# A list scheduler writes the order of all engines up to LayerNorm 1, and part of the second modulation is summed beside the FFN's first blocks

## The chip, the cores and the metric

The kernel runs on one core of a Trainium2 chip. Its time is the device time of one execution in microseconds, the median over runs. The engines of the core are named as in the profile: PE (TensorE, matrix products and transposes, with PEld for its weight loads), DVE (VectorE), ACT (ScalarE), POOL (GpSimd) and SP (SyncE, which issues all DMA transfers here). Each engine takes its instructions in the order in which the program lists them for it, and waits at an instruction whose inputs are not there.

## The reference

One layer of a diffusion transformer, in float32, for 256 latent tokens and 256 context tokens of width 2048. A conditioning vector gives six modulation vectors of width 2048 each (`w_ada` is 2048 x 12288, 100 MB). With one layer, the context only gives keys and values.

```python
sh1, sc1, g1, sh2, sc2, g2 = ada_mods(c, w_ada[layer], b_ada[layer])
csh1, csc1, ... = ada_mods(c_ctx[None, :], w_ada[layer], b_ada[layer])
qa, ka, va, qb, kb, vb = mixer_qkv(modulate(x, sh1, sc1), w_in[layer], ..., rope)
...
heads = concatenate([window_sink_attention(qa, ka, va, kac, vac, sink_logit[layer]),
                     global_attention(qb, kb, vb, kbc, vbc)], axis=-1)
x = layer_norm(DN_ALPHA * x + g1 * (heads @ w_out[layer]), ln1_g[layer], ln1_b[layer])
x = layer_norm(DN_ALPHA * x + g2 * swiglu(modulate(x, sh2, sc2), w_gate[layer], w_up[layer],
                                         w_down[layer]), ln2_g[layer], ln2_b[layer])
```

There are 16 query heads of 128 (8 windowed with a sink, 8 global with normalised queries and keys), 4 key/value heads, and an FFN of width 5632.

## The kernel before

**Products.** Every large product is made of three float32r matmuls (`mm3`, lines 130 to 133): a number is split into a rounded part `hi` and a rest `lo`, and hi x hi, hi x lo and lo x hi are summed. Weights come as raw float32 tiles of [128, 4 x 512] (1 MB) by SP; ACT rounds them (`hi`, line 121), DVE subtracts (`lo`, line 122), each 1024 columns at a time. A raw tile sits in one of six buffers up to LayerNorm 1 (four of `wraw`, two of `araw`), four afterwards. Inputs are split in the same way: `uh`/`ul` (modulated input), `oTh`/`oTl` (attention output), `u2h`/`u2l` (FFN input), `hTh`/`hTl` (FFN hidden).

**Modulation.** Modulation vectors are w_ada^T silu(c) in two ways. On PE, `ada_steps` multiplies raw float32 tiles by the conditioning columns into a bank `adaps` (line 230; a float32 matmul is two records in the trace), ACT copies it, and a tiny product with `sel` (line 253, the column step) turns rows into per-partition columns. On DVE, `ada_vector_steps` multiplies and adds raw tiles into an accumulator (line 204), 512 or 1024 columns at a time, and PE sums the partitions with a product with `ones` (line 268 for the gate g1 or g2, line 602 for columns).

**Stages.** (1) The input's 16 k-chunks of 128 are taken in groups of 1, 1, 2, 4 and 8 (`GROUPS`). `prep(g)` loads both halves of w_ada for the group, makes shift and scale, transposes x and ctx (line 351), modulates (line 355), and splits; `in_steps(g)` multiplies with w_in in six blocks of 512 columns and adds to q, k and v. `merge` interleaves the steps of group g with `prep(g+1)` evenly. Groups 0 and 1 load w_in as two tiles of 1536 columns each. (2) Keys, queries, and `attend_steps` for four head groups, merged with the rest of w_in, with the gate g1's DVE sums, and with `out_block`s, the products with w_out. (3) The second modulation feeds the FFN's input. It comes in four pieces of 512: m0 on DVE beside the last output blocks, m1 (shift and scale) on PE beside and after them (`first_modulation`), m2 and m3 on DVE beside the FFN's first blocks. (4) LayerNorm 1, then `z_part` transposes and modulates two k-chunks at a time. The FFN's gate and up blocks f = 0 to 5 are first done for k-chunks 0 to 7 only (`first_half`, 24 steps of 24 matmuls; the sums are put aside in `spill`) while m2 and m3 are summed; then they are finished, then f = 6 to 10. (5) The down projection, LayerNorm 2.

**What sets the order.** Lists are merged in Python, and from there the tile framework's own scheduler orders each engine's instructions, SP's included. Only two places are `manual_schedule` regions, where an engine takes the order of the code: ACT and DVE at the very start, and DVE, ACT and PE from the last output block to the FFN's first step.

## Time and profile before

| what | value |
|---|---|
| median of 3 runs | 1188.52 us (1187.82 to 1192.65) |
| profiled execution, its own time | 1189.62 us |
| its span, first to last instruction | 1187.8 us |
| granted PE clock, mean | 0.992 |
| read from HBM over the span | 289.91 MB |

The trace has several views. The table of stages gives each engine's busy time in a stretch of the span, with the number of instructions, the granted PE clock (1.00 is full), the mean busy share of the 16 DMA engines, and GB/s. The chain of waits goes back from the last instruction to what released it, piece by piece. The timeline has one row for each instruction or run of like ones: start, length, engine, line, operation, out<-in, count, and in brackets the idle time before it and what ended it. SPq rows are DMA issues. Matmul records are as long as a matmul's whole passage through the array, so two of them overlap; what one costs is the distance between starts.

### The profile page before, as it was taken

To read this page: it belongs to the slowest core of one execution; us is meant where nothing else is said; L and a number is where in the kernel's file an instruction comes from. 1 tells how busy PE (TensorE), PEld (TensorE's weight loads), DVE (VectorE), ACT (ScalarE), POOL (GpSimd) and SP (SyncE) were. 2 spreads that over 40 slices of the span, in tenths; PEclk is the share of its full clock that TensorE was granted. 3 is DMA by queue.
4 is the path that set the end of the run, shared out by engine and by line. 5 is a ranking of instruction groups with operands and counts; after the bars stand their busy time and mean duration, and the time that the engine had idled before them with its cause. 6 is when DMAs were issued, how large, how long until landed. Compare 5 with 4: busy or idle time off the path is not lost.

```text
span 1187.8 us, 14248 instructions
## 1 busy us (share of the span) xinstructions
PE 1158.3 (98%) x5527; PEld 916.4 (77%) x5527; DVE 800.4 (67%) x1026; ACT 530.3 (45%) x762; POOL 21.1 (2%) x43
## 2 busy tenths in 40 slices
PE   8999899999999999999999999999999999999995
PEld 7666578867777768888888888888888888888884
DVE  3763289998867888775776564544545778676556
ACT  2443142668675245445544444444444434343340
POOL 1100000000000010100000000000000000000000
PEclk9999999999999999999999999999999999999997
DMA  9999878853565969998675555565565888877541
GB/s 300 375 390 375 333 272 311 297 203 108 171 214 205 309 231 348 335 314 291 212 230 177 182 196 190 180 205 183 180 208 184 313 317 318 288 256 253 200 139 71
DMA packets 150137, 292.93 MB, mean 247 GB/s; under 512 B 5515, under 2 KB 20267, under 8 KB 147765
## 3 DMA queue, kind: packets, MB, share of 16 engines
q1 hardware_dynamic: 150070, 292.03, 70.8%
q8 instruction: 43, 0.70, 0.2%
q14 instruction: 24, 0.20, 0.0%
HBM read 289.91 MB, written 2.10 MB: 246 GB/s over the span
## 4 chain that ended last, share of the span: by engine, by line
PE 92%; DVE 3%; DMA 2%; ACT 1%; SPq 1%; issue 0%; DVEq 0%; ACTq 0%
PE acc L132 27%; PE acc L133 27%; PE acc L131 27%; PE adaps L230 3%; PE wk L537 2%; DMA raw<-in_w_ada_dram 2%; PE wk L525 1%; DVE lo L122 1%; PE wk L820 1%; PE wk L131 1%; PE wk L133 1%; PE wk L132 1%; PE wk L268 1%; SPq L101 1%; DVE xt L927 0%; PE wk L602 0%
## 5 line engine op out<-in xcount | busy, mean ns | idle before, releaser
L122 DVE TENSOR_TENSOR lo<-raw,hi 128x1024 fp32r<-128x1024 f32 x344 | 415.9, 1217 | 252.1 <-ACT hi L121 247.8
L121 ACT CAST hi<-raw 128x1024 fp32r<-128x1024 f32 x344 | 358.0, 1048 | 470.5 <-PE acc L133 406.2
L131 PE MATMUL acc<-hi,u2h 128*128 128x512 f32 x704 | 275.9, 392 | 0.8 <-ACT u2h L782 0.7
L133 PE MATMUL acc<-hi,u2l 128*128 128x512 f32 x704 | 274.9, 391 | 1.3 <-DVE u2l L783 1.3
L132 PE MATMUL acc<-lo,u2h 128*128 128x512 f32 x704 | 274.7, 390 | 0.0
L133 PEld LDWEIGHTS acc<-hi,u2l 128*128 128x128 f32 x704 | 132.6, 188 | 29.3 <-DVE u2l L783 1.7
L131 PEld LDWEIGHTS acc<-hi,u2h 128*128 128x128 f32 x704 | 132.6, 188 | 28.2 <-ACT u2h L782 1.2
L132 PEld LDWEIGHTS acc<-lo,u2h 128*128 128x128 f32 x704 | 132.6, 188 | 27.0
L131 PE MATMUL acc<-hi,hTh 128*128 128x512 f32 x344 | 135.5, 394 | 0.0
L133 PE MATMUL acc<-hi,hTl 128*128 128x512 f32 x344 | 134.1, 390 | 0.0
L132 PE MATMUL acc<-lo,hTh 128*128 128x512 f32 x344 | 134.0, 390 | 0.0
L204 DVE SCALAR_TENSOR_TENSOR adav<-raw,cs,adav 128x512 f32<-128x512 f32 (+1 forms) x112 | 109.5, 977 | 13.1 <-DMA raw<-in_w_ada_dram 11.5
L132 PE MATMUL acc<-lo,uh 128*128 128x512 f32 x256 | 102.0, 399 | 2.4 <-DVE lo L122 2.4
L131 PE MATMUL acc<-hi,uh 128*128 128x512 f32 x256 | 99.5, 405 | 2.8 <-ACT hi L121 2.8
L133 PE MATMUL acc<-hi,ul 128*128 128x512 f32 x256 | 101.4, 396 | 0.0
L132 PEld LDWEIGHTS acc<-lo,hTh 128*128 128x128 f32 x344 | 64.6, 188 | 14.3 <-issue 1.0
L131 PEld LDWEIGHTS acc<-hi,hTh 128*128 128x128 f32 x344 | 64.6, 188 | 14.3 <-issue 1.0
L133 PEld LDWEIGHTS acc<-hi,hTl 128*128 128x128 f32 x344 | 64.6, 188 | 13.2
L131 PEld LDWEIGHTS acc<-hi,uh 128*128 128x128 f32 x256 | 47.5, 189 | 18.9 <-ACT hi L121 6.5
L132 PEld LDWEIGHTS acc<-lo,uh 128*128 128x128 f32 x256 | 48.6, 190 | 15.4 <-DVE lo L122 5.0
L133 PEld LDWEIGHTS acc<-hi,ul 128*128 128x128 f32 x256 | 48.6, 190 | 9.9
L131 PE MATMUL acc<-hi,oTh 128*128 128x512 f32 x128 | 50.9, 398 | 0.0
(182 smaller groups left out, 1041.8 us busy)
## 6 DMA issues: line engine op xcount, KB each, us to landing
raw<-in_w_ada_dram SPq DMA_DIRECT2D x72, 1024.0 KB, 6.9
raw<-in_w_gate_dram SPq DMA_DIRECT2D x44, 1024.0 KB, 5.0
raw<-in_w_up_dram SPq DMA_DIRECT2D x44, 1024.0 KB, 5.0
raw<-in_w_down_dram SPq DMA_DIRECT2D x44, 1024.0 KB, 5.4
raw<-in_w_ada_dram SPq DMA_DIRECT2D x48, 512.0 KB, 5.3
raw<-in_w_in_dram SPq DMA_DIRECT2D x18, 1024.0 KB, 7.5
raw<-in_w_out_dram SPq DMA_DIRECT2D x16, 1024.0 KB, 5.0
raw<-in_w_in_dram SPq DMA_DIRECT2D x4, 768.0 KB, 7.6
```

Of the source, the lines that this page charges most:

```text
L101: nc.sync.dma_start(rv.rearrange("p (k n) -> p k n", k=nk), w[k0 * P : (k0 + nk) * P, c0 : c0 + width].rearrange("(k p) n -> p k n", p=P),)
L121: nc.scalar.copy(hi[:, :n], raw[:, s : s + n])
L122: nc.vector.tensor_tensor(lo[:, :n], raw[:, s : s + n], hi[:, :n].bitcast(F32), op=ALU.subtract)
L131: nc.tensor.matmul(ps, lhsT=xh, rhs=w[0], start=first, stop=False)
L132: nc.tensor.matmul(ps, lhsT=xh, rhs=w[1], start=False, stop=False)
L133: nc.tensor.matmul(ps, lhsT=xl, rhs=w[0], start=False, stop=last)
L204: nc.vector.scalar_tensor_tensor(a[:, c : c + piece], raw[:, j * w + c : j * w + c + piece], cs[:, g * nk + j, 2:3], a[:, c : c + piece], ...
L230: nc.tensor.matmul(st["ps"][32 * j : 32 * j + 32, :width], lhsT=cs[:, k, 2 - 2 * i : 34 - 2 * i], rhs=raw[:, c * width : (c + 1) * width], ...
L268: nc.tensor.matmul(ps, lhsT=ones, rhs=sb[:, s : s + NB], start=True, stop=True)
L525: nc.tensor.transpose(t_ps[:, k * P : (k + 1) * P], pr[:, k * P : (k + 1) * P], ident)
L537: nc.tensor.matmul(o_ps, lhsT=v, rhs=pTs[t][k // 2][:, k % 2, :], start=k == 0, stop=k == 3)
L820: nc.tensor.transpose(ps[:, j * P : (j + 1) * P], hh[:, j * P : (j + 1) * P], ident)
```

## The change

The order of SP, PE, ACT, DVE and POOL from the start to LayerNorm 1 is now made by a list scheduler in the kernel, `Flow`. The code no longer issues instructions there; it adds steps with an engine, a cost in ns, the steps that must be done first, the buffers taken and given back, and a due time (`F.at`). `run` goes through modelled time: whenever an engine is free, the ready step with the earliest due time starts, if its buffers are free. Then all steps are issued in the order of their modelled starts, in one `manual_schedule` region of all five engines, which now reaches from the start to the FFN's first step.

With it come these differences:

- The bank `adaps` is gone; PE's scratch banks `wk` are four, not three. Column sums use them (line 476 now, the column step is line 505).
- Groups 0 and 1 load w_in in four tiles of 512, 1024, 1024 and 512 columns.
- Attention goes by pairs of heads: one `pT` of 512 columns for each head's transposed probabilities (one ACT copy, not two), values of 256 columns for a pair.
- The output blocks are (0,) for column block 0, (0, 1) for 1 to 3, (1,) for 0, then (2, 3) for all four; the number of DVE additions goes from 16 to 10.
- m1: only the shift is summed on PE (16 matmuls, after the last output block, line 1161). The scale is summed on DVE (16 sums of 512 columns, line 329) beside the FFN's first blocks; its columns are made by 4 tiny matmuls (line 1185).
- The FFN's blocks 0 to 2 are first done for k-chunks 0 to 3 only (`ONE_F`), 3 to 7 for chunks 0 to 7 (`SPLIT_F` = 8, not 6): 26 steps. The first 6 need only z_part(0) and z_part(2); after five of them come m1's scale and z_part(4) and (6). m2 and m3 stand beside the next 19 steps.
- PE's warm-up matmuls are 56 single steps with the last due time, so that they fill free time (44 before).

```diff
-SPLIT_F = 6
+T2K = 5
+WARM = 56
+ONE_F = 3
+SPLIT_F = 8
...
+class Flow:
...
+    SAME = {"SP": 0, "PE": 0, "ACT": 60, "DVE": 80, "POOL": 80}
+    OTHER = {"SP": 2000, "PE": 270, "ACT": 90, "DVE": 90, "POOL": 150}
...
+    def add(self, eng, ns, fn, after=(), take=(), give=(), at=None):
+        s = Step()
+        s.eng, s.ns, s.fn, s.take, s.give = eng, ns, fn, take, give
+        s.after = [a if isinstance(a, tuple) else (a, 0) for a in after if a is not None]
+        s.rank = (self.at if at is None else at, len(self.steps))
...
+    def run(self):
...
+            for e in self.ENGINES:
...
+                for item in sorted(ready[e]):
+                    s = item[1]
...
+                    pools = [next((p for p in b.pools if self.room[p] > 0), None) for b in s.take]
+                    if None in pools or any(self.room[p] < pools.count(p) for p in pools):
+                        continue
...
+                    s.start, end = now, now + s.ns
+                    free[e] = end
...
+                    order.append(s)
...
+        for s in order:
+            s.fn()
...
-    wk_ps = ctx.enter_context(tc.tile_pool(name="wk_ps", bufs=3, space=PSUM))
+    wk_ps = ctx.enter_context(tc.tile_pool(name="wk_ps", bufs=4, space=PSUM))
...
-    ada_ps = ctx.enter_context(tc.tile_pool(name="ada_ps", bufs=1, space=PSUM))
...
+    region = tc.manual_schedule(engines={ET.DVE, ET.Activation, ET.PE, ET.Pool, ET.SP})
+    region.__enter__()
...
+    def dma_ns(nbytes, row):
+        return nbytes / (390 if row >= 2048 else 340 if row >= 1024 else 290)
...
+            a = F.add("ACT", 60 + 0.87 * n, cast, [ld], [hl])
+            b = F.add("DVE", 60 + 1.06 * n, rest, [a], give=[raw])
...
+        after = [deps[0], (deps[1], 200), ready[0], (ready[1], 400)]
+        return F.add("PE", 681 * len(cols), fn, after, [ps] if first else [], [hl])
...
+            for i, (b0, m) in enumerate(((2, 1), (0, 2), (3, 2), (5, 1))):
+                F.at = bs[0] + (bs[1] - bs[0]) * i / 4
+                piece, = flow_weights(w_in, k0, 1, b0 * NB, m * NB, where)
...
+            v = F.add("PE", 1800, values, g, [o_ps], [pT, *kv_room[w]])
...
+    for _ in range(WARM):
+        F.add("PE", 225, lambda: warm(wps, 1), at=1e6)
...
+                nc.tensor.matmul(bank1.t[32 * j : 32 * j + 32, :], lhsT=cs[:, g * 4 + j, 2:34],
+                                 rhs=raw.t[:, j * NB : (j + 1) * NB], start=g == 0, stop=g == 3)
...
+    F.run()
...
+    groups = [1 if f < ONE_F else EARLY_G if f < SPLIT_F else 0 for f in range(FFN // NB)]
...
+    scales = ada_vector_steps((4 * D + NB,), NB, lambda: late_sums[1]()[:, :NB], second_scales)
...
     run(first_half[:1])
     region.__exit__(None, None, None)
-    later[0]()
+    second_shifts(adav1)
+    run(merge(first_half[1 : 2 * ONE_F - 1], scales))
     combine(1)
     z_part(4)
     z_part(6)
     cutoff = len(first_half) - 2
-    run(merge(first_half[1:cutoff], side))
+    run(merge(first_half[2 * ONE_F - 1 : cutoff], side))
```

In what follows a row has the line of the code, the operation, out<-in, the shape and a count. First place: SP's loads for the last two input groups. Before:

```order
L101 DMA raw<-in_w_in_dram 128x4x512
L101 DMA raw<-in_w_ada_dram 128x4x512 x6
L101 DMA raw<-in_w_in_dram 128x4x512 x2
L101 DMA raw<-in_w_ada_dram 128x4x512 x2
L336 DMA xt<-in_x_dram 128x2x512
L339 DMA cxt<-in_ctx_dram 128x2x512
L101 DMA raw<-in_w_ada_dram 128x4x512 x4
L101 DMA raw<-in_w_in_dram 128x4x512
L101 DMA raw<-in_w_ada_dram 128x4x512 x2
L101 DMA raw<-in_w_in_dram 128x4x512 x4
```

Now:

```order
L421 DMA raw<-in_w_in_dram 128x4x512
L421 DMA raw<-in_w_ada_dram 128x4x512 x6
L542 DMA cxt<-in_ctx_dram 128x2x512
L312 DMA g1b<-in_b_ada_dram 1x2048
L367 DMA cosA<-in_rope_cos_dram 128x2x128
L368 DMA sinA<-in_rope_sin_dram 128x2x128
L369 DMA gq<-in_q_norm_g_dram 128x128
L370 DMA gk<-in_k_norm_g_dram 128x128
L371 DMA sinkb<-in_sink_logit_dram 128x8
L421 DMA raw<-in_w_in_dram 128x4x512
L421 DMA raw<-in_w_ada_dram 128x4x512 x2
L421 DMA raw<-in_w_in_dram 128x4x512
```

The w_ada tiles of the last group no longer come four and two between w_in tiles, but six and then two and two, and the constants for rotation and normalisation stand here, where they were loaded in group 1 before. Up to the last w_ada pair of the input SP issues 48.70 MB before and 49.75 MB now.

Second place: PE at the third column step of four rows, where the first half of the last group gets its modulation (`sel` in these rows). Before:

```order
L133 MATMUL acc<-hi,ul 128x512
L230 MATMUL adaps<-raw,cs 32x512 x24
L253 MATMUL wk<-sel,ada 128x4 x4
L351 MATMUL wk<-ident,xt 128x128 x8
L351 MATMUL wk<-ident,cxt 128x128 x8
L131 MATMUL acc<-hi,uh 128x512 x2
```

Now:

```order
L223 MATMUL acc<-hi,ul 128x512
L476 MATMUL wk<-raw,cs 32x512 x16
L505 MATMUL wk<-sel,ada 128x4 x4
L562 MATMUL wk<-ident,xt 128x128 x8
L562 MATMUL wk<-ident,cxt 128x128 x4
L476 MATMUL wk<-raw,cs 32x512 x8
L562 MATMUL wk<-ident,cxt 128x128 x4
L221 MATMUL acc<-hi,uh 128x512
```

Column sums stand in smaller runs between the projection matmuls. At the next such step, the last one, 336 projection matmuls stand ahead on PE before, and 366 now.

Third place: PE from the last output block to the FFN's first matmul. Before:

```order
L133 MATMUL acc<-hi,oTl 128x512
L230 MATMUL adaps<-raw,cs 32x512 x20
L707 MATMUL acc<-ident 128x128 x8
L776 MATMUL wk<-ident,xt 128x128 x4
L707 MATMUL acc<-ident 128x128 x6
L776 MATMUL wk<-ident,xt 128x128 x4
L253 MATMUL wk<-sel,adav 128x4 x4
L131 MATMUL acc<-hi,u2h 128x512
```

Now:

```order
L223 MATMUL acc<-hi,oTl 128x512
L1161 MATMUL wk<-raw,cs 32x512 x16
L1038 MATMUL acc<-ident 128x128 x8
L1215 MATMUL wk<-ident,xt 128x128 x4
L1038 MATMUL acc<-ident 128x128 x6
L1215 MATMUL wk<-ident,xt 128x128 x4
L1177 MATMUL wk<-sel,adav_3716 128x4 x4
L221 MATMUL acc<-hi,u2h 128x512
```

and DVE at the same place, before:

```order
L122 TENSOR_TENSOR lo<-raw,hi 128x1024 x2
L256 TENSOR_TENSOR sh_133<-wk,bcol 128x8
L257 SCALAR_TENSOR_TENSOR sc_134<-wk,bcol 128x8
L122 TENSOR_TENSOR lo<-raw,hi 128x1024
L783 TENSOR_TENSOR u2l<-uf_3756,u2h 128x512
```

Now:

```order
L212 TENSOR_TENSOR lo<-raw,hi 128x1024 x2
L1222 TENSOR_TENSOR u2l<-uf_3787,u2h 128x512
L1180 TENSOR_TENSOR sh_132<-wk,bcol 128x8
L212 TENSOR_TENSOR lo<-raw,hi 128x1024 x2
L1222 TENSOR_TENSOR u2l<-uf_3803,u2h 128x512
```

All 16 column sums that are left of m1 (each two records in the trace) stand in one run, and the first u2l has moved ahead of a pair of lo casts.

More of the change, by code (lines that the diff above doesn't have):

```diff
@@ L1 @@
+import heapq
 import math
@@ L261, in ada_rows, with rows_from @@
[L261 to L271 removed]
+    def rows_from(sb, dst, s):
+        ps = wk_bank()
+        nc.tensor.matmul(ps, lhsT=ones, rhs=sb[:, s : s + NB], start=True, stop=True)
+        return lambda: nc.scalar.copy(dst[:, s : s + NB], ps)
@@ L372, in in_part, with flow_block @@
+                a = F.add("ACT", 60 + 240 * nj, cast, [p], rooms if j0 == 0 else [])
+                b = F.add("DVE", 60 + 330 * nj, rest, [a], give=[uf])
+                u[k0, s][1].append((a, b))
+    evacs = {}
+    def flow_block(g, b, chunks):
         k0, ng = GROUPS[g]
@@ L694, in out_block, with warm @@
-        return last_block if last else block
-    def soon(steps, offset):
-        def step(s):
-            with tc.high_priority(offset=offset):
-                s()
-        return [lambda s=s: step(s) for s in steps]
-    def warm(n):
+            outs[n, t] = F.add("DVE", 710, add, [ends[t], outs[n, t]], give=[ps])
+            if gs[-1] == 3:
+                outs[n, t] = F.add("DVE", 2160, rest, [outs[n, t], gates[n]])
+        for t in range(NT):
+            finish(t)
+    def warm(wps, n):
```

1041 lines of the change are left out of this document (667 added, 374 removed).

## The prediction

> **What bounds the kernel now.** I read the page first, then a table of stages, then the chain of waits, then the timeline where the stages differ.
>
> ```profile
> span 1187.8 us, 14248 instructions
> PE 1158.3 (98%) x5527; PEld 916.4 (77%) x5527; DVE 800.4 (67%) x1026; ACT 530.3 (45%) x762; POOL 21.1 (2%) x43
> ```
>
> TensorE (PE) looks full, but a matmul's recorded length overlaps the next one's, so the 98% cannot say how much is lost. Two views can: the weight loads (PEld) by stage, whose records do not overlap, and counted work against elapsed time. In the stage table the columns are length, then busy time of PE, PEld, DVE and ACT with instruction counts, then granted clock, DMA share and GB/s.
>
> ```profile
> 24.00:105.00 81.00, 80.96 (x500) 53.71 (x498) 49.90 (x74) 27.11 (x43) 4.69 (x13) 1.00 1.01 373
> 105.00:146.50 41.50, 36.02 (x189) 23.39 (x185) 15.15 (x20) 12.83 (x21) 0.00 (x0) 0.96 0.93 353
> 157.50:420.00 262.50, 262.40 (x1191) 196.49 (x1190) 224.90 (x370) 146.09 (x309) 0.55 (x3) 1.00 0.64 225
> 420.00:442.00 22.00, 19.90 (x125) 13.90 (x125) 18.74 (x36) 11.75 (x18) 3.97 (x5) 0.92 0.73 248
> 442.00:560.00 118.00, 118.00 (x543) 98.19 (x541) 87.80 (x78) 55.64 (x68) 6.10 (x7) 1.00 0.93 328
> ```
>
> In the FFN PEld is busy 98.19 of 118 us, 83%; from 105 to 146.5 it is 56%, and PE itself is idle 5.5 us. So there are two regimes: an input phase in which loads (373 GB/s at a DMA share of 1.01) and PE are nearly equal, and everything after it, which is PE alone.
>
> The chain of waits prices one projection matmul and the small pieces of PE work (start, us, piece):
>
> ```profile
> 35.86 3.59 PE adaps L230 x64
> 99.75 5.33 PE adaps L230 x48
> 146.49 1.06 PE wk L253 x8
> 244.87 0.44 PE wk L525 x4
> 260.29 3.44 PE wk L537 x8
> 387.45 0.99 PE adaps L230 x8
> 407.21 1.88 PE wk L602 x16
> 420.09 4.43 PE adaps L230 x40
> 845.16 0.87 PE wk L820 x8
> 889.57 0.87 PE wk L820 x8
> ```
>
> Between the last two lie one FFN block's 192 matmuls: (44.41 - 0.87) / 192 = 0.2268 us each. A 128x128 transpose costs 0.11 us.
>
> **The input phase.** Its landmark is the fourth column step of four rows (L253 at 146.49): with it the last four k-chunks of the input get their modulation. In the order before, 336 projection matmuls stand ahead of it, in the order of the change 366. PE's first real work and its first projection matmul:
>
> ```profile
> 12.37 1.96 PE L230 MATMUL adaps<-raw,cs 128*32 128x128 f32 x64
> 21.20 1.20 PE L131 MATMUL acc<-hi,uh 128*128 128x512 f32 x4
> ```
>
> Work ahead of the landmark, before: 336 x 0.2268 = 76.2; column sums 2 x 1.96 + 3.59 + 192 records x 0.111 = 28.8; 48 transposes 5.3; three column steps about 1.8. Sum 112.1 us, in 146.5 - 12.4 = 134.1 us: 22 us idle. Of it 21.20 - 12.37 - 1.96 = 6.9 us lie before the first projection matmul; from 105 on PE has no work for 5.5 us on record, and the clock at 0.96 of 41.5 us costs 1.7 more; the rest are short waits. Why PE is dry from 105 on:
>
> ```profile
> 106.67 12.79 SPq L101 DMA_DIRECT2D raw<-in_w_ada_dram  x4
> 129.47 0.37 SPq L101 DMA_DIRECT2D raw<-in_w_in_dram  x1
> ```
>
> ```profile
> 125.00:130.00 5.00, 5.00 (x32) 3.05 (x34) 1.37 (x2) 0.00 (x0) 0.00 (x0) 1.00 0.19 73
> 130.00:135.00 5.00, 3.71 (x34) 0.90 (x26) 0.00 (x0) 0.33 (x1) 0.00 (x0) 1.00 0.89 299
> 135.00:140.00 5.00, 3.71 (x11) 2.72 (x12) 2.36 (x2) 1.67 (x2) 0.00 (x0) 0.81 1.05 408
> ```
>
> ```profile
> 134.67 2.00 ACT L121 CAST hi<-raw 128x1024 fp32r<-128x1024 f32 x2 [17.74 <-DMA raw<-in_w_in_dram]
> 135.77 0.73 PE L131 MATMUL acc<-hi,uh 128*128 128x512 f32 x2 [2.05 <-ACT hi L121]
> ```
>
> SP issues nothing for 10 us up to 129.47: all six raw buffers hold w_ada tiles that PE reaches only after a block of projection matmuls. The loader falls to 73 GB/s, and the next w_in tile is then late for ACT and PE. A row that makes this dearer: the 2.05 us wait is followed by a granted clock of 0.81 from 135 to 140. The Trainium skill ("TensorE: Matmul & The Clock Gate", HAM oscillation — how this bites in real kernels) says that PE must be idle for some 3.4 us before its clock is halved; this case's trace shows a shorter wait doing it. By that rule short waits left in the new order would be free of a clock loss, and the forecast a microsecond or two lower.
>
> **The change, term 1: the new order of this phase.** The scheduler sums a w_ada pair of the last groups in pieces of 8 matmuls or 16 between projection matmuls, where the old order had 24 and 23 in a row, so buffers return sooner; and it puts x's first transposes ahead of the first sums, where before they came after ten warm-up matmuls. Its landmark can come at 12.4 + work + idle. Work is 112.1 + 30 x 0.2268 = 118.9 us. For idle I take 5 us at the start, 4 for the short waits and 2 from 105 on, 11 in all: 142.3 us. The loader allows it: 49.75 MB are issued up to the last w_ada pair (48.70 before); 7.0 MB are in by 24 us, and the rest at 373 GB/s takes 115 us, to 138.6, and some 2 us for sum and copy: 140.6. The old order reaches the same 366 matmuls at 146.5 + 6.8 = 153.3. **Gain 11.0 us.** Bounds: idle stays at 22 us, 0, and with 1.05 MB more ahead of the last pair at 373 GB/s a loss of 2.8; only the 5 us at the start stay, 17.
>
> **Term 2: attention and output projection (157 to 420).** This is where the scheduler could only do harm. Work: 768 + 384 - 336 projection and 96 score matmuls x 0.2268 = 206.8; values 27.5 (64 records); 192 transposes 21.1; second modulation 3.0 + 1.9; sum 260.3 of the 273.5 us from the landmark, without mask and gate rows. So at most 13 us are open, most of them those small pieces. The values become 64 matmuls of half the width, the same columns. I take **0**, from -10 to +5.
>
> **Term 3: half of the m1 sums leaves PE.** Before, 24 records run between output blocks (three pieces like 387.45) and 40 after the last (420.09). The order after has 32 records, all after the last block. That takes 3 x 0.99 = **3.0 us** off PE's path. The 8 records fewer in the tail give nothing, since a DVE chain ends there:
>
> ```profile
> 419.70 0.39 PE L133 MATMUL acc<-hi,oTl 128*128 128x512 f32 x1
> 426.03 0.55 DVE L646 TENSOR_SCALAR xt<-xt,mv,ly 128x512 f32<-128x512 f32 x1
> 429.79 0.50 PE L131 MATMUL acc<-hi,u2h 128*128 128x512 f32 x1
> 431.81 0.79 PE L133 MATMUL acc<-hi,u2l 128*128 128x512 f32 x1 [1.29 <-DVE u2l L783]
> 441.61 0.50 PE L131 MATMUL acc<-hi,u2h 128*128 128x512 f32 x1 [0.75 <-ACT u2h L782]
> ```
>
> The 10.1 us from the last output matmul to the first FFN matmul are evacuation, statistics, normalisation, transposes, modulation: unchanged. If this cover went, the 3.5 us of sums left there would show.
>
> **Term 4: the FFN's start.** In the new order the first u2l stands behind two lo casts, not three, which removes most of the 1.29 us; the second now stands behind two more, so I count 0.5. The 0.75 us at 441.61 goes, since that step moves back by four blocks. New is a wait: after 120 FFN matmuls (27.2 us) PE's queue holds the columns of the scale sums (L1185), and behind them z_part(4), z_part(6) and every later FFN matmul. DVE must by then have done some 12 lo casts, 16 sums of 512 columns, six normalisations and two u2l.
>
> ```profile
> L122 DVE TENSOR_TENSOR lo<-raw,hi 128x1024 fp32r<-128x1024 f32 x344 | 415.9, 1217 | 252.1 <-ACT hi L121 247.8
> L204 DVE SCALAR_TENSOR_TENSOR g1b<-raw,cs,g1b 128x1024 f32<-128x1024 f32 x32 | 40.3, 1277 | 0.0
> ```
>
> ```profile
> L204 DVE SCALAR_TENSOR_TENSOR adav<-raw,cs,adav x112: 735/752/1286, 320.5 to 1092.3; 128x512 f32<-128x512 f32 x64, 128x1024 f32<-128x1024 f32 x48
> ```
>
> 12 x 1.217 + 16 x 0.752 + six at 0.55 + two at 0.69 = 31.3 us from 426.6, against PE's arrival at 429.8 + 27.2: 457.9 against 457.0. I charge 1 us. **Term 4: 0**, from -5 to +2.5.
>
> **Term 5: denser first blocks.** The two last modulations (16 MB) now lie beside 19 first-half steps of 5.44 us, not 21: 35 x 1.0486 MB in 103 us, 355 GB/s, where 442 to 560 shows 328 at a share of 0.93, so a share of 1.0, which the input phase held. DVE: 38 x 1.217 + 32 x 1.277 = 87 of 103 us. I charge 1 us, and 8 more records like those of L602 (1.88 / 16 each) 0.9: **-1.9**, from 0 to -7. The two further blocks split in halves cost 0: ACT copies and DVE additions, with ACT at 47% and DVE at 74% in that row.
>
> **Sum:** 11.0 + 0 + 3.0 + 0 - 1.9 = 12.1 us. The profiled execution took 1189.6 us for a span of 1187.8; it becomes 1177.5. It lies 1.1 above the median of the three runs, so I forecast **1176 us**.
>
> **Rivals.**
>
> *The loader stays the bound.* Four w_in loads of 768 KB become eight of 256 and 512 KB, each in a buffer for 1 MB.
>
> ```profile
> raw<-in_w_in_dram SPq DMA_DIRECT2D x6, 512.0 KB, 7.2
> ```
>
> A buffer is taken for 7.2 us whatever it holds; four more loads over six buffers cost 4 x 7.2 / 6 = 4.8 us of loading, and if the dry spell of 125 to 135 stays too (4.7 us, the missing share there) the landmark comes at 150.1, a gain of 3.2 in place of 11.0: 1184 us. For it: PE and loader are within 2 us in my own term. Against it: the share of 1.01 with 512 KB loads among the rest. The Trainium skill ("DMA: Bandwidth & Descriptors", Bandwidth) asks for loads of 1 MiB or more and so speaks against these pieces. The trace so far does not bear a loss out.
>
> *Denser blocks starve the FFN.* Terms 4 and 5 at their ends, 4 to 5 us each worse: near 1185. For it: a buffer ring of four and no slack on DVE. Against: the input phase moved 373 GB/s for 81 us.
>
> *The fixed order stalls attention.* Each engine now takes exactly what the table says. If a pair's probabilities are late, PE stands at their transposes with ready work behind them.
>
> ```profile
> 205.79 0.40 PE L133 MATMUL wk<-kTh,qTl 128*128 128x512 f32 x1
> 215.14 0.60 PE L525 MATMUL wk<-ident,pr 128*128 128x128 f32 x4
> ```
>
> From a pair's last score matmul to its first transpose pass 9.3 us here. The new order covers the first pairs with about 10 us and the later ones with 7 to 8.5 (for one, values 1.7 and 24 matmuls 5.4). Short by 2 us at each of 16 pairs: 32 lost, 1176 + 32 = 1208. It decides from 12.1 / 16 = 0.8 us per pair. Against it: the later pairs have no gate sums of DVE's in the way, which delayed this one.
>
> **How the numbers follow.** Forecast 0.65, loader 0.11, FFN 0.10, attention 0.14. What a measurement can tell from no change is 0.5%, 5.9 us: faster is below 1182.6. The forecast gives 0.63 of faster, the loader 0.05, the FFN 0.07: 0.75. Within: 0.12. Slower, nearly all from attention: 0.13. The range runs from term 1 at its upper bound (-6), terms 2 and 4 half way to theirs (-3.7) and term 5 at nothing (-1.9), about 1164, up past the loader's and the FFN's cases by some 3 us, 1188.
>
> **What would show it.** Right: the fourth column step near 142; no hole in SP's issues of 10 us; last output matmul near 406 (419.7); first FFN matmul near 416 (429.8); the first hh transposes near 587 (598.65). Wrong: PE waiting for `pr` (term 2), for a hi or lo tile before 160 (term 1), at L1185 or a later z_part (term 4), or a DMA wait from 460 to 560 (term 5).

## The result and the profile after

The changed kernel took 1190.82 us in the median of 12 runs (1187.43 to 1195.69), the kernel before 1189.26 us (12 runs, 1187.82 to 1192.65): a ratio of 1.0011, 95% interval 0.9995 to 1.0026. No difference of 0.5% or more, where a gain of 12 us was forecast.

The profiled execution is the longest of its 12, 1195.69 us, with the lowest granted clock in the mean, 0.988. The spread goes with the clock: the five runs at 0.990 or lower took 1191.8 to 1195.7 us, the seven above 1187.4 to 1191.0. So this trace shows a dear execution; the experiments repeat the same code in other executions.

The first lines of the page and the table of stages (columns as in the prediction's stage table). The cuts at 24, 105 and 560 us are the same times as there; the others follow the fourth column step and the last output matmul:

```profile
span 1193.9 us, 14384 instructions
PE 1159.9 (97%) x5591; PEld 937.1 (78%) x5591; DVE 817.2 (68%) x1052; ACT 531.3 (45%) x746; POOL 24.4 (2%) x44
```

```profile
24.00:105.00 81.00, 79.12 (x507) 56.29 (x506) 47.91 (x70) 27.41 (x43) 0.00 (x0) 0.96 0.96 349
105.00:153.50 48.50, 44.64 (x248) 28.24 (x246) 19.32 (x25) 16.05 (x24) 8.38 (x16) 1.00 1.03 391
163.50:418.50 255.00, 251.27 (x1195) 204.62 (x1194) 215.15 (x358) 140.91 (x281) 1.99 (x4) 0.99 0.59 205
418.50:440.50 22.00, 19.76 (x111) 15.17 (x111) 16.66 (x37) 9.02 (x13) 0.95 (x1) 0.84 0.78 287
440.50:560.00 119.50, 116.79 (x523) 94.78 (x522) 97.50 (x91) 56.53 (x72) 6.56 (x8) 1.00 0.94 334
```

Two things are new. The clock lost in the input phase is now lost before 105 us (0.96) and not after it, and at the FFN's start it is 0.84 where it was 0.92. And the last row has PE short of work for 2.7 of 119.5 us, where it had none missing in 118.

**Input phase.** The timeline of PE (start, us, piece, and in brackets the wait ahead of it), then the stage table for five short stretches:

```profile
77.65 0.50 PE L221 MATMUL acc<-hi,uh 128*128 128x512 f32 x1 [0.87 <-ACT hi L439]
78.91 0.50 PE L222 MATMUL acc<-lo,uh 128*128 128x512 f32 x1 [0.76 <-DVE lo L442]
...
134.20 0.50 PE L221 MATMUL acc<-hi,uh 128*128 128x512 f32 x1 [1.69 <-ACT hi L439]
...
153.44 0.95 PE L505 MATMUL wk<-sel,ada 128*128 128x4 f32 x8
```

```profile
76.00:80.00 4.00, 2.37 (x13) 1.04 (x6) 2.31 (x2) 2.58 (x3) 0.00 (x0) 0.92 1.05 407
80.00:85.00 5.00, 5.00 (x21) 4.63 (x20) 3.24 (x6) 3.17 (x5) 0.00 (x0) 0.50 1.05 402
95.00:100.00 5.00, 5.00 (x24) 4.15 (x23) 2.89 (x4) 0.27 (x1) 0.00 (x0) 1.00 0.64 247
100.00:105.00 5.00, 5.00 (x40) 1.86 (x39) 1.88 (x3) 0.00 (x0) 0.00 (x0) 1.00 0.16 27
130.00:135.00 5.00, 3.01 (x22) 1.02 (x21) 2.23 (x3) 4.55 (x10) 5.00 (x12) 1.00 1.05 394
```

At 77 PE waits for a w_in tile while the loader is full (share 1.05, 407 GB/s). Then the clock is halved (0.50 from 80 to 85), and PE is late. From 89.00 to 103.07 SP issues nothing, and the loader drops to 27 GB/s from 100 to 105; at 134 PE is dry again. SP's issues, and the column sums on PE that end the hole:

```profile
89.00 1.17 SPq L537 DMA_DIRECT2D xt<-in_x_dram  x1
103.07 0.37 SPq L421 DMA_DIRECT2D raw<-in_w_ada_dram  x1
```

```profile
101.08 3.64 PE L476 MATMUL wk<-raw,cs 128*32 128x512 f32 x32
```

The old order had two such holes, the one from 119 to 129 us and an earlier one:

```profile
77.25 13.38 SPq L101 DMA_DIRECT2D raw<-in_w_ada_dram  x6
100.81 1.23 SPq L101 DMA_DIRECT2D raw<-in_w_in_dram  x2
```

The new order has lost the second and kept the first: SP waits for a buffer whose w_ada tile PE sums only behind a block of 60 projection matmuls (87.28 to 101.08 us). PE's lateness lengthens the hole but does not make it. m1_on_pe, an experiment below with the same input phase and a granted clock of 1.00 up to the column step, has it too, with the sums 4.1 us earlier:

```profile
89.50 1.17 SPq L537 DMA_DIRECT2D xt<-in_x_dram  x1
98.93 0.37 SPq L421 DMA_DIRECT2D raw<-in_w_ada_dram  x1
```

```profile
96.94 3.64 PE L476 MATMUL wk<-raw,cs 128*32 128x512 f32 x32
```

In the ten profiles with the new order the hole is 9.4 to 14.1 us long from issue to issue.

The fourth column step comes at 153.44 us with 366 projection matmuls ahead: where the old order had got to the same work, at 153.3.

**Attention.** Work ran 264.8 us from there to the last output matmul at 418.20 (old order 266.4, from 153.3). One stall is new. DVE waits for a w_ada tile of the second modulation, and the maxima of the scores stand behind it; PE then waits for their probabilities:

```profile
350.37 2.60 DVE L329 SCALAR_TENSOR_TENSOR adav<-raw,cs,adav 128x1024 f32<-128x1024 f32 x2 [2.10 <-DMA raw<-in_w_ada_dram]
352.89 1.88 DVE L814 TENSOR_REDUCE m<-wk 128x1 f32<-128x512 f32 x3
```

```profile
355.80 3.68 PE L339 MATMUL wk<-g1b,ones 128*128 128x512 f32 x4 [2.04 <-ACT pr L826]
```

The granted clock behind it is 0.66 from 355 to 360, which costs 1.7 us more.

**Between output projection and FFN.** PE's rows, all pieces that are not output matmuls:

```profile
418.51 3.64 PE L1161 MATMUL wk<-raw,cs 128*32 128x512 f32 x32
422.09 2.05 PE L1038 MATMUL acc<-ident 128*128 128x128 f32 x16
423.97 0.27 PE L1215 MATMUL wk<-ident,xt 128*128 128x128 f32 x1
426.49 0.55 PE L1215 MATMUL wk<-ident,xt 128*128 128x128 f32 x3 [2.24 <-DVE xt L976]
426.87 2.17 PE L1038 MATMUL acc<-ident 128*128 128x128 f32 x12
...
429.69 1.71 PE L1177 MATMUL wk<-sel,adav 128*128 128x4 f32 x8
431.25 0.77 PE L221 MATMUL acc<-hi,u2h 128*128 128x512 f32 x1
```

The last output matmul is 1.5 us earlier than before, the first FFN matmul 1.5 us later. With fewer sums to do, PE runs out and waits 2.24 us; 12 warm-up records then take 2.17 us instead of the 1.50 of a full clock, and the first FFN matmuls start 0.42 us apart, not 0.227.

The chain on DVE does not start at the last output matmul. It starts when tile 0 of the last output block is done, first before and then now:

```profile
414.69 0.69 DVE L665 TENSOR_TENSOR oacc<-oacc,acc 128x512 f32<-128x512 f32 x1 [2.48 <-PE acc L133]
```

```profile
414.55 0.69 DVE L1020 TENSOR_TENSOR oacc<-oacc,acc 128x512 f32<-128x512 f32 x1 [2.50 <-PE acc L223]
```

The matmul that releases it is the 24th of the last block's 48 before, and the 30th now: the scheduler put a step of six matmuls of the other tile ahead. So the block began 1.5 us earlier (407.40, before 408.95) and DVE's chain only 0.1 us earlier.

**FFN.** From the first FFN matmul to the last of the gate and up phase it took 498.4 us before (429.79 to 928.15) and 502.2 now (431.25 to 933.5).

### The profile page after: what moved, and what is told of

It is laid out like the page before. It is cut to its first block, busy times and chain, and to the rows that moved or that the text cites. A ratio compares the mean times of both kernels' runs of the same rounds, so it can differ in the third digit from the quotient of the medians.

```text
span 1193.9 us, 14384 instructions
## 1 busy us (share of the span) xinstructions
PE 1159.9 (97%) x5591; PEld 937.1 (78%) x5591; DVE 817.2 (68%) x1052; ACT 531.3 (45%) x746; POOL 24.4 (2%) x44
## 4 chain that ended last, share of the span: by engine, by line
PE 80%; DVE 8%; DMA 8%; ACT 2%; issue 1%; POOL 0%; SPq 0%; DVEq 0%; ACTq 0%; POOLq 0%
PE acc L222 23%; PE acc L223 23%; PE acc L221 23%; DMA raw<-in_w_ada_dram 3%; DMA raw<-in_w_in_dram 3%; DVE adav L329 2%; PE wk L855 2%; DVE lo L212 1%; PE wk L476 1%; PE acc L1038 1%; DMA lgb<-in_ln_b_dram 1%; PE wk L1259 1%; PE wk L844 1%; PE wk L339 1%; DMA raw<-in_w_gate_dram 1%
## 5 line engine op out<-in xcount | busy, mean ns | idle before, releaser
L212 DVE TENSOR_TENSOR lo<-raw,hi 128x1024 fp32r<-128x1024 f32 x262 | 317.8, 1223 | 215.3 <-ACT hi L211 211.7
L211 ACT CAST hi<-raw 128x1024 fp32r<-128x1024 f32 x262 | 273.5, 1053 | 363.8 <-PE acc L223 306.9
L439 ACT CAST hi<-raw 128x1024 fp32r<-128x1024 f32 (+1 forms) x82 | 83.6, 1030 | 143.3 <-PE acc L223 74.7
L329 DVE SCALAR_TENSOR_TENSOR adav<-raw,cs,adav 128x512 f32<-128x512 f32 (+1 forms) x128 | 121.4, 948 | 13.2 <-DMA raw<-in_w_ada_dram 11.0
L442 DVE TENSOR_TENSOR lo<-raw,hi 128x1024 fp32r<-128x1024 f32 (+1 forms) x82 | 97.5, 1195 | 37.0 <-ACT hi L439 36.7
L221 PE MATMUL acc<-hi,uh 128*128 128x512 f32 x256 | 103.8, 406 | 2.7 <-ACT hi L439 2.6
```

The source lines that it names most:

```text
L211: nc.scalar.copy(hi[:, :n], raw[:, s : s + n])
L212: nc.vector.tensor_tensor(lo[:, :n], raw[:, s : s + n], hi[:, :n].bitcast(F32), op=ALU.subtract)
L221: nc.tensor.matmul(ps, lhsT=xh, rhs=w[0], start=first, stop=False)
L329: nc.vector.scalar_tensor_tensor(a[:, c : c + piece], raw[:, f : f + piece], cs[:, g * (G4 * NB // w) + j, 2:3], a[:, c : c + piece], op0= ...
L439: nc.scalar.copy(hl.hi[:, :n], raw.t[:, s : s + n])
L442: nc.vector.tensor_tensor(hl.lo[:, :n], raw.t[:, s : s + n], hl.hi[:, :n].bitcast(F32), op=ALU.subtract)
```

## The experiments

One table for all, from each run's profile (us). The second column's line is the fourth column step: with 336 projection matmuls ahead in the old order (add 6.8 for the same work), with 366 in the new. The last column is the median with the ratio to the kernel before in the same runs.

| kernel | 4th step | last output matmul | first FFN matmul | last gate/up | span | median, ratio [95%] |
|---|---|---|---|---|---|---|
| before | 146.5 | 419.7 | 429.8 | 928.1 | 1187.8 | 1189.3 |
| before_again | 148.8 | 421.8 | 431.9 | 928.8 | 1188.5 | 1190.2, one run |
| changed | 153.4 | 418.2 | 431.3 | 933.5 | 1193.9 | 1190.8, 1.0011 [0.9995, 1.0026] |
| half_ada | 144.8 | 407.2 | 418.4 | 920.2 | 1180.7 | 1182.5, one run |
| m1_on_pe | 149.0 | 416.2 | 426.3 | 925.3 | 1184.8 | 1186.4, 0.9986 [0.9972, 1.0001] |
| tail_warm | 151.6 | 412.3 | 423.0 | 925.6 | 1186.2 | 1188.7, 1.0004 [0.9986, 1.0022] |
| m0_lag | 150.1 | 410.4 | 424.4 | 927.5 | 1187.1 | 1190.0, 1.0016 [1.0003, 1.0028] |
| dense_blocks | 152.9 | 419.0 | 429.0 | 924.5 | 1184.0 | 1185.8, one run |
| combo | 155.1 | 417.4 | 427.9 | 923.8 | 1183.3 | 1182.3, 0.9957 [0.9940, 0.9974] |
| combo2 | 155.4 | 416.9 | 431.1 | 929.9 | 1189.7 | 1185.9, 0.9984 [0.9966, 1.0003] |
| combo3 | 151.3 | 413.6 | 424.6 | 919.4 | 1178.9 | 1180.8, 0.9939 [0.9920, 0.9958] |
| landing | 150.5 | 415.2 | 426.5 | 921.3 | 1180.7 | 1185.6, 0.9965 [0.9951, 0.9979] |

m1_on_pe and dense_blocks have 24 records of column sums ahead of the last output matmul (2.7 us), combo, combo3 and landing 16, combo2 8. Landmarks are those of one profiled execution; the medians are over other executions too, and combo2's profiled one (1191.5 us) is the second longest of its 12.

### half_ada: is the loader the bound of the input phase?

```
-            nc.sync.dma_start(room.t..., w[k0 * P : (k0 + nk) * P, c0 : c0 + width]...)
+            if little:                        # the scale's tile of a pair, c0 > 0
+                nc.sync.dma_start(room.t[:, 0:8], w[k0 * P : (k0 + 1) * P, c0 : c0 + 8])
+                return
...
-                    fn(g, 1, r1, 0, nk)
+                    fn(g, 1, r0, 0, nk)
```

> Of each pair of w_ada tiles for the first modulation only the shift's is loaded; the scale's is replaced by a load of 8 columns, and its column sums read the shift's tile (a wrong scale). Order and PE work are those of the changed kernel; 9 MB less are loaded up to the fourth column step. Theory A (the input phase waits on the loader: 153.6 us for that step because weights land late): the step comes at 138 to 146 us, PE's waits on hi, lo and w_ada between 70 and 145 go, and the granted clock stays at 1.0 there. Rival B (the order itself leaves PE waiting on PE, ACT and DVE work, whatever the loader does): 151 to 154 us.

Measured: 144.80 us.

```profile
75.00:90.00 15.00, 15.00 (x87) 11.95 (x78) 10.10 (x15) 10.20 (x17) 0.00 (x0) 1.00 1.01 360
90.00:110.00 20.00, 20.00 (x112) 12.87 (x111) 8.32 (x10) 1.99 (x2) 0.00 (x0) 1.00 0.71 242
110.00:130.00 20.00, 18.10 (x114) 11.46 (x114) 6.20 (x10) 7.79 (x15) 4.91 (x16) 1.00 0.67 236
```

Theory A holds for the step: PE is busy from 75 to 110 without a gap, and the clock stays at 1.00. Not all waits go, as it had said: 1.9 us of idle PE stay between 110 and 130. The edit takes out more than the 9 MB expected: 15 of the 32 w_ada tiles shrink to 8 columns, 15.7 MB, and 38.5 MB are read up to the step where the changed kernel reads 53.3. Those loads cost this order 4 to 11 us (149.0 to 155.4 in the other executions); the lower figure is against m1_on_pe, whose clock was 1.00 up to the step as well. But the step does not come at the 131.3 us of pure work (12.4 + 118.9): 13.5 us stay without these loads.

### m1_on_pe: the second part undone

```
-    for g in range(4):
-        F.at = END + 60
-        raw, ld = flow_load(w_ada, g * 4, 4, 3 * D + NB, NB, W)
+    for i, g in [(i, g) for i in range(2) for g in range(4)]:
+        F.at = END + 22 if i == 0 and g < 3 else END + 60
+        raw, ld = flow_load(w_ada, g * 4, 4, (3 + i) * D + NB, NB)
...
-ONE_F = 3
-SPLIT_F = 8
+ONE_F = 0
+SPLIT_F = 6
```

> The second part undone inside the new order: the shift and the scale of the second group both summed on PE (24 records between output blocks, 40 after the last), blocks of the FFN's first half as before. Theory A (the second part costs more than it saves: it leaves a gap and half the clock at the FFN's start and a wait before z_part(4)): the first FFN matmul stays within 1.5 us of 431.3, the clock from 420 to 440 is above 0.90, the wait at the scale columns goes, and the whole is 3 to 5 us faster than the changed kernel, 1186 to 1188 us. Rival B (the second part is worth the 3 us of PE records that it takes off the path, the loss lies in the order): 2 to 4 us slower than the changed kernel, near 1194 us.

Measured: first FFN matmul 10.1 us after the last output matmul (13.05 in the changed kernel, 10.1 before), gate and up phase 499.0 us (502.2), 1186.38 us, within the range of theory A. (The first FFN matmul's own time, 426.3, is not, since the input phase was 4.4 us earlier than in the changed kernel's profile.) The new order alone thus gives 0.14%, with an interval from 0.28% to nothing: a gain of the first part is not shown. That the second costs more than it takes off PE is, if narrowly: the two kernels' ratios differ by 0.25%, and their intervals overlap by 0.06%. The stall at 350 us was there too (2.00 us of PE for pr).

### tail_warm: the cover of DVE's chain

```
-    warm(wps, 8)
+    warm(wps, 16)
```

> Only edit: 16 instead of 8 warm-up products behind the last column sums before LayerNorm 1's first transposes. Theory A (PE idles 2.2 us there, its clock is halved, and the first FFN matmuls run at 0.43 us instead of 0.227): first FFN matmul at 429 to 430 us when the last output matmul is at 418.2, no clock below 0.95 from 420 to 440, 2 to 3.5 us faster than the changed kernel. Rival B (the DVE chain alone sets the FFN's start and the half clock costs nothing): no change.

```profile
416.23 3.84 PE L1038 MATMUL acc<-ident 128*128 128x128 f32 x32
419.91 0.27 PE L1215 MATMUL wk<-ident,xt 128*128 128x128 f32 x1
420.62 0.55 PE L1215 MATMUL wk<-ident,xt 128*128 128x128 f32 x3 [0.44 <-DVE xt L976]
421.01 1.50 PE L1038 MATMUL acc<-ident 128*128 128x128 f32 x12
...
422.98 0.50 PE L221 MATMUL acc<-hi,u2h 128*128 128x512 f32 x1
```

The wait falls from 2.24 to 0.44 us, 12 warm-up records take 1.50 us again, and the FFN starts 10.6 us after the last output matmul, not 13.05. The granted clock was 1.00 from 414 to 434 us. Theory A holds for this place, with a reserve: half_ada has the changed kernel's code here and the same wait of 2.24 us, kept a clock of 1.00, and starts the FFN 11.3 us after the last output matmul. So the wait itself costs 0.6 us against tail_warm and the lost clock 1.8, and one execution cannot show that the 16 products are what kept the clock. In the total the expected 2 to 3.5 us are not shown: the median is 2.2 us below the changed kernel's, but the ratios to before, 1.0004 and 1.0011, differ by 0.8 us, and their intervals overlap.

### m0_lag: sums behind the maxima

```
-    a = flow_vector((3 * D, 4 * D), NB, adav, (END - 14, END + 24))
+    a = flow_vector((3 * D, 4 * D), NB, adav, (END - 14, END + 24), 6000)
...
-                last = F.add("DVE", 1200, ..., [ld, last], give=[room])
+                last = F.add("DVE", 1200, ..., [(ld, -lag), last], give=[room])
```

> Only edit: the scheduler reckons 6 us more until the second modulation's w_ada tiles can be summed, so the sums stand behind the maxima of the scores on DVE, not ahead. Theory A (DVE's wait for a w_ada tile at 350 us held the maxima, the exponentials and PE): no wait of PE for pr between 340 and 370, from the fourth column step to the last output matmul 261 to 262 us instead of 264.6, 3 to 4 us faster than the changed kernel. Rival B (the scores' banks or ACT hold PE there anyway): the stretch stays at 264 to 265 us.

The stall was gone: 260.4 us from the column step to the last output matmul. But tail_warm, without the 6 us, took 260.7 us in its execution. Over all profiles, the stall stands in four of the five without the 6 us (the changed kernel, half_ada, m1_on_pe, dense_blocks; PE waits 1.7 to 2.0 us) and in none of the five with it. Against 260.5 us, the records between output blocks taken off, it costs 2 to 3 us where the clock stays at 1.00 (half_ada, dense_blocks) and some 4 where it drops (the changed kernel, m1_on_pe). And the FFN's start lost what was won: 14.0 us after the last output matmul, with PE waiting 3.33 us for xt. DVE's chain stood later against PE, since the last block's tile 0 ends here with its 36th matmul, two steps of the other tile ahead of it. That the postponed sums led the scheduler to this order was not tried by itself. The median is no better than the changed kernel's.

### dense_blocks: scale sums or denser blocks?

m1_on_pe with the FFN's blocks of the changed kernel:

```
-ONE_F = 0
-SPLIT_F = 6
+ONE_F = 3
+SPLIT_F = 8
...
+    run(first_half[1 : 2 * ONE_F - 1])
     combine(1)
     z_part(4)
```

> m1_on_pe with the FFN's first blocks as in the changed kernel (three blocks of one group, five of two, z_part(4) after five steps, the two last modulations beside 19 steps): only the scale sums on DVE and their wait are gone. From the first FFN matmul with u2h to the last with u2l it took 498.3 us before, 499.0 in m1_on_pe, 502.3 in the changed kernel, 502.6 and 503.1 in tail_warm and m0_lag. Theory A (term 4: the scale sums hold z_part(4), and with it PE): 499 to 500 us. Rival B (term 5: the denser blocks starve): 501.5 to 503 us.

Measured: 495.5 us, below both ranges. The denser blocks cost nothing; the scale sums on DVE, with their four loads and what waits for them, cost all of it, some 7 us. Of these, 1.5 to 1.7 us are clock: the kernels with the sums lost that much granted clock in this phase, dense_blocks none. Sums, loads and the wait were not tried apart. The same stretches, first of tail_warm (sums on DVE, first FFN matmul at 422.98), then of dense_blocks (429.03):

```profile
450.00:460.00 10.00, 8.92 (x49) 7.32 (x47) 6.69 (x8) 7.69 (x14) 2.73 (x4) 1.00 0.93 342
460.00:470.00 10.00, 9.10 (x33) 7.03 (x32) 9.60 (x9) 3.70 (x5) 0.00 (x0) 0.83 0.90 308
470.00:480.00 10.00, 9.78 (x43) 7.46 (x41) 5.95 (x5) 4.31 (x6) 0.00 (x0) 1.00 0.84 286
```

```profile
460.00:470.00 10.00, 10.00 (x46) 8.28 (x45) 8.31 (x9) 6.76 (x11) 0.00 (x0) 1.00 0.72 243
470.00:480.00 10.00, 10.00 (x46) 8.29 (x45) 8.55 (x7) 4.80 (x6) 0.00 (x0) 1.00 1.05 403
```

A full stretch has 8.29 us of weight loads. With the sums on DVE 10 us at a time lack 0.8 to 1.3 us of them for thirty us; in the second of the three part of it is the clock of 0.83.

### before_again, combo, combo2

> The kernel before, unchanged, for a second execution with a profile. It shows how far a landmark moves between executions without an edit: the fourth column step stood at 146.5 us with 336 projection matmuls ahead, 153.3 us for 366. If it comes again within 1 us, the new order's 149.0 to 153.4 us in four executions is a gain of about 2 us in the mean; if the old order moves as much (149 to 153), the input phase gained nothing.

The column step came at 148.82 us, 2.3 us later than in the first profile. So the old order moves too: 153.3 and 155.6 us for the work of 366 matmuls, 154.5 in the mean; the new order's eight executions with unchanged input phase lie at 149.0 to 155.4, 152.3 in the mean. Its gain there is about 2 us in the mean, less than the scatter, and so not shown.

combo joins the three edits: 2 of 8 tiles of the sums ahead of the last output block (`g < 2` where m1_on_pe has `g < 3`), FFN blocks as before, and m0_lag's 6 us for the first six tiles only (`-lag * (g < 6)`).

> The new order with what the first four runs point to: the second group's sums all on PE, 16 records between output blocks and 48 after the last, FFN blocks as before, and the first six tiles of the second modulation reckoned 6 us later. Theory A (the loss sat in DVE's wait at 350 us, in the cover of the tail and in the scale sums, 3.6 at times, 3 and 4 us): last output matmul 412 to 415 us, first FFN matmul 10 us later, gate and up phase 499 us; 1182 to 1185 us, ratio to before 0.994 to 0.997. Rival B (losses of this kind move elsewhere): 1187 to 1190 us.

1182.25 us, ratio 0.9957 [0.9940, 0.9974]: 0.4% faster than the kernel before, within theory A's range, although its profiled execution had a late input phase (155.1 us, and with it the last output matmul at 417.4, past the 412 to 415 expected). The first FFN matmul came 10.5 us later, and the gate and up phase took 495.9 us, not 499. In combo2 one tile stands ahead and part of DVE's residual is put later:

```
-        F.at = END + 22 if i == 0 and g < 2 else END + 60
+        F.at = END + 22 if i == 0 and g < 1 else END + 60
...
-                outs[n, t] = F.add("DVE", 2160, rest, [outs[n, t], gates[n]])
+                outs[n, t] = F.add("DVE", 2160, rest, [outs[n, t], gates[n]], at=F.at + 11.5 * (n == 2))
```

> As combo, with 8 records between output blocks and 56 after the last, and the last part of the third output block's residual on DVE put behind the last block's lo casts, so that tile 0 of the last block is done earlier. Theory A: last output matmul 1 us earlier than in combo, DVE's chain and the first FFN matmul 0.9 us earlier, 0.5 to 1 us faster. Rival B (the tail's w_ada loads come too late for 56 records): PE waits for them, and it is as slow as combo or slower.

Rival B: PE waits 1.01 us for the last w_ada tile at 423.55, comes to the transposes at 426.44, 2.7 us after DVE's chain has ended, waits 1.51 us for u2h, and starts the FFN 14.2 us after the last output matmul. 1185.93 us.

### combo3 and landing

combo3 is combo with dense_blocks' edit.

> combo with the FFN's first blocks of the changed kernel (three of one group, five of two, z_part(4) after five steps), which in dense_blocks made the gate and up phase 495.5 us long where m1_on_pe had 499.0. Theory A (the later z_part(4) also clears the waits for u2l and u2h at the FFN's start): 1180 to 1182 us, no wait of PE over 1 us between 425 and 560. Rival B (combo's own 495.9 us shows that m1_on_pe's 499.0 was that execution's): as combo, 1182 to 1184 us.

1180.81 us in six runs, ratio 0.9939 [0.9920, 0.9958], the fastest kernel of the study: 8.6 us below the one before in the medians of the same runs, 7.3 us by the ratio. The gate and up phase took 494.8 us, and no wait of PE over 1 us stands between 425 and 560 (one of 1.05 us for u2h ends at 424.56). Against combo (two sets of runs with other runs of before, 0.9957) the gain is within the intervals.

landing adds 1.5 us to what the scheduler reckons for a load:

```
-            a = F.add("ACT", 60 + 0.87 * n, cast, [ld], [hl])
+            a = F.add("ACT", 60 + 0.87 * n, cast, [(ld, -LAND * (w is w_in))], [hl])
...
-                prev = F.add("PE", 2 * ns1 + 420, both, [l0, l1, prev], ...)
+                prev = F.add("PE", 2 * ns1 + 420, both, [(l0, -LAND), (l1, -LAND), prev], ...)
```

> As combo3; in addition the scheduler reckons 1.5 us more between a w_in or w_ada tile's load and its first use. In all nine executions with the new order PE waits for a w_in tile's hi or lo near 77 us and again between 130 and 145 us, where the scheduler has planned their landing earlier than they land. Theory A (those waits, and what the late PE then costs the loader, are the 3 to 9 us by which the fourth column step comes after the planned 146.0): the step comes at 148 to 150.5 us, with no wait near 77 us over 0.5 us, and the whole is 1 to 3 us faster than combo3. Rival B (the loader is simply full, and a later use only moves PE's wait): 151 to 156 us, and no faster than combo3.

The step came at 150.5 us and the wait for hi near 77 was gone, but PE waited 1.06 us for the copy of column sums there instead, and the median was 4.8 us above combo3's, 1185.64 us (the intervals just overlap). Theory A's step, at the edge of its range, and rival B's total: a later first use moved PE's wait. One profile cannot tell whether the step is steadier. The expectation gives the wait near 77 us to every execution of the new order; half_ada had none there.

## Why the prediction was wrong

**Term 1 failed in the idle time.** The step was "For idle I take 5 us at the start, 4 for the short waits and 2 from 105 on, 11 in all: 142.3 us". The chip shows 13.5 us with 15.7 MB less to load (half_ada) and 17.7 to 24.1 with the full loads (149.0 to 155.4 less 131.3), against the 22 worked out for the old order. Counted with the prediction's own price for each piece of PE work, the idle time of each part is:

| us of idle time | start (12.4 to 24) | 24 to 105 | from 105 to the step |
|---|---|---|---|
| forecast | 5 | 4 | 2 |
| old order, two profiles | 6.8 to 7.0 | 5.1 to 5.3 | 9.2 to 11.7 |
| changed kernel | 5.3 | 10.5 | 6.8 |
| m1_on_pe | 5.2 | 6.5 | 6.5 |
| half_ada | 5.7 | 4.5 | 3.7 |

The start came as forecast. The short waits grew, and from 105 on some 3 us went, not 7. Nothing in the trace of before supported that the waits would be that short; I had worked out how long the loader takes in the mean (140.6 us) and read it as permission. I had also found only one of SP's two holes in the trace of before. The other, from 89.78 to 100.81, cost that order little, since the loader still had work (share 1.04 or more up to 100 us, 0.69 from 100 to 105). The new order kept it, and there the share falls to 0.58 from 95 to 100 in m1_on_pe, and in the changed kernel to 0.64 and then 0.16. Lost clock comes on top, but is not the cause of the miss: m1_on_pe had none up to the step and still came 6.7 us after the 142.3. That the hole costs these microseconds is read from the traces; no run removes it alone.

The gain was about 2 us in the mean, not 11. That is 9 of the 12 us forecast. The rival "the loader stays the bound" gave 150.1 us for the step, which is inside what was measured; it had 0.11. That its number fits is partly luck. It kept the loader's dry spell of 125 to 135, which went (share 0.92 and 1.05 there in the changed kernel), and had no earlier one, and it took a buffer to be held "7.2 us whatever it holds", where the loads of 1 MB in the same part of the trace took 11.5 and 10.1 us. Its own mechanism, the small w_in pieces, was not tried alone, so what is shown is the loader, not the pieces. The rule of the Trainium skill that the prediction weighed there ("DMA: Bandwidth & Descriptors", Bandwidth: loads of 1 MiB or more) is thus neither borne out nor refuted.

**Term 2 (0, from -10 to +5) and term 3 (3.0).** Together they were worth more than 3.0 up to the last output matmul: 260.4 and 260.7 us from the step where DVE did not hold the scores, 266.4 and 266.2 before. With the stall at 350 us 264.8. Not all of it reaches the FFN: up to the end of DVE's chain it is 268.9 (tail_warm) and 269.7 us (m0_lag), before 273.3 and 273.1, a gain of some 4 us. The rival of a fixed order that stalls attention had the right kind of wait (PE waiting for pr) and the wrong place: not short cover at each of 16 pairs, but one DVE instruction that waits for a load with the maxima behind it, at 2 to 4 us when it comes.

**The tail: "The 8 records fewer in the tail give nothing".** The chain on DVE did end at the same time (426.4 us, before 426.6), as said, but the last output matmul had come 1.5 us earlier. The 10.1 us from the last output matmul to the FFN, taken as unchanged, became 13.05. Two things make up the 3.0 us, as large as term 3's forecast gain. DVE's chain started 1.4 us later against the last output matmul, since tile 0 ended with the 30th matmul and not the 24th. The rest is PE's clock: half_ada, with the same late start and the same wait of 2.24 us but no lost clock, took 11.3 us. The prediction named what would show if the cover went, and did not ask what PE does when the cover gets shorter, nor which matmul releases the chain.

**Term 4 (0, from -5 to +2.5) was mis-sized, and its wait was one link further.** PE comes to the scale columns at 460.22 us with nothing to wait for; DVE was through at 459.5, near the 457.9 worked out. What is late stands behind them, on POOL and ACT. The timeline of the changed kernel, engine by engine (DVE, POOL, ACT, PE):

```profile
456.39 3.11 DVE L329 SCALAR_TENSOR_TENSOR adav<-raw,cs,adav 128x512 f32<-128x512 f32 x4 [0.44 <-DMA raw<-in_w_ada_dram]
```

```profile
461.23 0.95 POOL L306 MEMSET adav<- 128x1024 f32 x1 [28.76 <-PE wk L1185]
...
463.83 0.20 POOL L903 TENSOR_TENSOR mB<-mB,sh 128x4 f32<-128x4 f32 x1
```

```profile
464.07 1.48 ACT L1219 ACTIVATE uf<-wk,mB,mA 128x256 f32<-128x256 f32 x3 [2.17 <-POOL mB L903]
...
467.55 1.05 ACT L211 CAST hi<-raw 128x1024 fp32r<-128x1024 f32 x1
```

```profile
460.22 0.95 PE L1185 MATMUL wk<-ones,adav 128*128 128x2 f32 x8
...
468.65 0.73 PE L221 MATMUL acc<-hi,u2h 128*128 128x512 f32 x2 [1.08 <-ACT hi L211]
470.28 0.50 PE L222 MATMUL acc<-lo,u2h 128*128 128x512 f32 x1 [0.89 <-DVE lo L212]
```

POOL forms mA and mB only after the scale columns, ACT waits 2.17 us for them, and the next casts of hi stand behind ACT's waiting instruction. PE runs dry, and stays short for some thirty us. I had named what is queued behind L1185 on PE, not what is queued on ACT. In dense_blocks POOL had mB thirty us earlier, and the loss is gone: 495.5 us against 502.2 to 503.1 in the three kernels with the sums on DVE and full loads. That this wait is the larger part of the loss is read from the trace: dense_blocks also takes the sums' time off DVE and their four loads out of this stretch.

```profile
431.13 1.06 POOL L903 TENSOR_TENSOR mB<-mB,sh 128x4 f32<-128x4 f32 x1
```

**Term 5 (-1.9) was too dear.** Denser blocks cost nothing: 495.5 us, and 494.8 in combo3, against 498.4 and 496.9 before.

**In sum**, against the old order: about 2 us from the input phase and 5.5 to 6 up to the last output matmul, given back by the tail (1.2 where the clock stays, 3.0 in the changed kernel's profile), by the scale sums (4 to 6 against before) and, in four of five executions, by the stall at 350 us (2 to 4). What is left is nothing that can be measured. combo3, which keeps the scheduler, sums the scale on PE again and has the stall's 6 us, is 0.6% faster than the kernel before.

## What to carry to other kernels

A bound that two engines share within a few per cent does not yield what an order saves in the mean: take the waits out of the trace one by one, and credit a new order only with those whose cause it removes. Work that fills a gap on TensorE beside a longer chain is not free to move: count what is left to fill the gap, and the clock after it, and find the instruction that starts the longer chain: the last one on TensorE need not be it. Where a wait is added, follow its consumers on every in-order engine up to the next matmul, not only the queue of the engine that waits.

## What the runs showed of the hardware that was not expected

Short waits halve PE's clock, and not each time. After waits of 0.87 and 0.76 us at 77 to 79 us the granted clock was 0.50 from 80 to 85 us; in half_ada a wait of some 2.2 us ahead of the FFN left it at 1.00; in combo3 one of 3.11 us at 131.60 us came with 0.77 from 130 to 145. The Trainium skill ("TensorE: Matmul & The Clock Gate", HAM oscillation — how this bites in real kernels) has some 3.4 us of idle time before the clock is halved; the trace of the changed kernel disagrees at 77 us.

In the twelve profiles the clock lost from 12.4 us to the end of the gate and up phase comes in equal portions: one or two at a place, 1.7 us each, which is half the clock for 3.4 us. Where they fall goes with much of the scatter of the input phase. In the eight executions of one input phase the fourth column step came at 149.0 us where no portion fell ahead of it (m1_on_pe), at 150.1 to 152.9 where two fell near 130 us, and at 153.4 to 155.4 where two fell near 80 us. Each loss stands behind short waits of PE, but m1_on_pe had waits of the same kind (0.77 us at 77.95, 1.86 at 130.37) and no loss. What decides is not shown.

The same code moves by several us between executions without any edit: the fourth column step from 149.0 to 155.4 us in eight executions of one input phase, and by 2.3 us in two of the old. A landmark of one profile is therefore known to 3 us or so in this stage, while the gate and up phase, counted from its first matmul, agrees within 1.3 us in four executions of one code (501.8 to 503.1) and within 1.5 us in two of the old (498.4 and 496.9).
